# Norm factors of a two-layer diffusion block: from per-token columns to a product with ones on all partitions

## The chip, the cores and the metric

The kernel runs on one core of one Trainium2 chip. The metric is device time in microseconds (us), the median of several executions. A core has engines that run side by side: TensorE (PE, with PEld for its weight loads) multiplies matrices, VectorE (DVE) and ScalarE (ACT) work elementwise, GpSimd (POOL) does little here, and DMA queues move data between HBM and the on-chip SBUF. Matmul results land in PSUM. Each engine takes its own instructions strictly in the order of the program and waits on semaphores for the others.

## The reference

Two layers work on 256 tokens x and 256 context tokens ctx, 1024 features each. A layer is a half feed-forward, a block of four mixers, and a second half feed-forward; each starts with an RMS norm that is scaled and shifted by vectors from an adaLN product. In the second layer ctx ends after the mixers' states.

```python
def rms_norm(x, g):
    xf = x.astype(jnp.float32)
    y = xf * lax.rsqrt(jnp.mean(xf * xf, axis=-1, keepdims=True) + EPS)
    return (y * g.astype(jnp.float32)).astype(x.dtype)

def modulate(h, shift, scale):
    return h * (1 + scale) + shift

def half_ffn(h, shift, scale, gate, g, wi, wo):
    return h + 0.5 * gate * swiglu(modulate(rms_norm(h, g), shift, scale), wi, wo)

def hybrid_layer(x, ctx, c, c_ctx, p, last):
    ...
    x = half_ffn(x, sx[0], sx[1], sx[2], p['ffn1_norm'], p['ffn1_wi'], p['ffn1_wo'])
    ctx = half_ffn(ctx, sc[0], sc[1], sc[2], p['ffn1_norm'], p['ffn1_wi'], p['ffn1_wo'])
    u_x = modulate(rms_norm(x, p['mix_norm']), sx[3], sx[4]) @ p['w_in']
    ...
    x = x + sx[5] * mix_tokens(u_x, rows, dirs_x, states_x, p)
    x = half_ffn(x, sx[6], sx[7], sx[8], p['ffn2_norm'], p['ffn2_wi'], p['ffn2_wo'])
    if not last:
        ...
    return x, ctx
# after both layers: rms_norm(x, final_norm)
```

One of the four mixers, the convolution, ends in a layer norm over 256 channels, whose variance is computed in the same way as the RMS norms.

## The kernel before

Activations lie with features on the 128 partitions: `x` is 8 tiles `x[m]` of 128 features by 512 tokens, the first 256 (a half, S = 256) of x and the other 256 of ctx. Products need fp32 accuracy, so each operand is split into a high part in the format fp32r and a low part that holds the rest: weights `raw` into `whi` (a cast on ACT, L165) and `wlo` (a subtraction on DVE, L166), normed activations into `yh` and `yl`. A product is then three matmuls (`mm3`, L177 to L179): high by high, low by high, high by low. Weights stream through two buffers of 128 x 2048 for `whi` and two for `wlo`, so that a cast waits until the matmuls that read the buffer last are done.

A stage ends with projections that update `x`: `part` (L479) does one tile m for a range of tokens and adds it to `x[m]`. For 512 tokens `project` holds back the tile m = 6 (KT - 2) and then goes by halves: m = 6 and 7 for the first 256 tokens, then m = 6 and 7 for the second. Both tiles lie in one weight buffer.

After each update ACT squares `x[m]` (L374) and DVE adds it to the sum `ss` (L378). The next stage's norm needs the factor 1 / root(mean + EPS) per token on all partitions:

- `rstd` brings the sum over the partitions into columns, one token per partition, by small fp32 matmuls with a two-column operand `mean` (L391 for the tiles 0 to 6, L392 for the last square).
- `rsqrt_cols` (L204 to L215) does a root from an integer first guess and three Newton steps, on tiles of 128x1 and 128x2.
- `bcast` multiplies the identity by each column (`diag`, L225) and takes a product with ones (L227), which leaves the factor in PSUM on all partitions.
- `norm_scale` (L416) makes `ny` from `x`, the scale `gs` and the factor; `norm_shift` makes `yh` on ACT (L423) and `yl` on DVE (L424).

The first half's statistics are hooked into the second half's matmuls, after RA/8 of the tile m = 6 and, for the spread, after RB/8 of the tile m = 7; the second half's come behind. Where only 256 tokens are left (`early` in `ffn`, the last boundary), the first two up-projections use `z` = x times scale, and the factor comes in afterwards (`late_act`, `zg` and `zv`, L544 and L546).

Five such boundaries are spoken of below, by the time of the trace: I (first feed-forward to mixers, layer 0, 412 us), II (mixers to second feed-forward, 619), III (to layer 1, 987), IV (first feed-forward to mixers, layer 1, 1361) and V (the last one, 256 tokens, 1494).

In the mixers, the input weights come in groups of columns: `k` (keys, 8 x 128 columns, half a buffer), `vg` (values and gates, 8 x 288, of which seven fit a buffer and the last goes into tiles of its own, `rest`), `q` and more. `group` loads and splits them ahead of their turn (`prio`). Products with `fm` have features, those with `tm` tokens on the partitions. The order of the instructions on each engine is set when the program is built: a scheduler places them by priority and its own estimate of when they are ready, and it's fixed from then on. So code that changes in one place shifts what stands beside what in others.

## Time and profile before

| | us |
|---|---|
| median of 3 runs | 1705.04 (1703.88 to 1705.18) |
| profiled execution | 1703.85 |
| its span in the profile | 1702.1 |
| PE busy | 1678.8 |
| DVE busy | 1193.8 |
| ACT busy | 575.8 |

The span is what the profile covers; the execution's own time is 1.75 us longer. A row of a timeline gives start, duration, engine, line, operation, tiles and how many were merged, and in brackets how long the engine had been idle before it and what ended that. Matmuls are pipelined: a duration of 0.28 us includes the way through the array, while the next starts 0.12 us later. An fp32 matmul appears as two records. The granted clock is that of TensorE, 1.00 for its full level of 2.4 GHz and 0.50 for 1.2 GHz.

### The profile page before, as it was taken

The page shows a single profiled execution, that of the slowest core. Times are in us where ns is not written, and L with a number is a line of the kernel's source. Part 1 is how long each engine was busy: PE and PEld are TensorE (multiplying, and loading weights), DVE is VectorE, ACT ScalarE, POOL GpSimd, SP SyncE. Part 2 cuts the span into 40 slices and gives each one's busy share as a digit, 9 for nine tenths or more (in the row PEclk, how much of TensorE's full clock was granted, in tenths as well). Part 3 has the DMA queues.
Part 4 walks back from the last instruction along what each step waited for, and adds up shares of the span by engine and source line. Part 5 has one row for each costly group of instructions (what it writes and reads, how often), then busy time and mean ns, then how long its engine had stood idle before and what let it go on. Part 6 is the DMA issues. An engine that isn't in the chain of part 4 may idle for free.

```text
span 1702.1 us, 23539 instructions
## 1 busy us (share of the span) xinstructions
PE 1678.8 (99%) x9650; PEld 1440.4 (85%) x9650; DVE 1193.8 (70%) x2077; ACT 575.8 (34%) x737; POOL 33.6 (2%) x59
## 2 busy tenths in 40 slices
PE   8999999999999999999999999999999998999998
PEld 5888888878888898888888898888878897899998
DVE  5799866896675678888669776654464678775555
ACT  3322212333532443222122242221233254554343
POOL 0000000010000000000000000000000000000010
PEclk9999999999999999999999999999999999999999
DMA  9555644533232235545445425444433234344552
GB/s 370 185 188 182 211 157 153 180 121 104 102 105 85 95 129 180 183 163 183 166 148 193 165 104 194 166 155 149 151 124 106 86 130 162 110 157 177 179 195 79
DMA packets 51452, 262.55 MB, mean 154 GB/s; under 512 B 6010, under 2 KB 10944, under 8 KB 28816
## 3 DMA queue, kind: packets, MB, share of 16 engines
q1 hardware_dynamic: 49968, 257.05, 42.9%
q0 software_dynamic: 1376, 4.00, 0.6%
q8 instruction: 75, 1.23, 0.3%
q14 instruction: 33, 0.27, 0.0%
HBM read 257.88 MB, written 3.15 MB: 153 GB/s over the span
## 4 chain that ended last, share of the span: by engine, by line
PE 92%; DVE 3%; DMA 2%; ACT 1%; issue 1%; SPq 0%; POOL 0%; DVEq 0%; ACTq 0%; POOLq 0%
PE psm L177 29%; PE psm L178 28%; PE psm L179 28%; DVE acc L316 1%; ACT whi L165 1%; DVE wlo L166 1%; DMA adaw<-in_ada_w_dram 1%; DMA pm<-in_k_pool_dram 1%; PE psa L979 1%; DMA vec<-in_vecs_dram 1%; PE psa L1216 0%; PE psa L1038 0%; PE psa L1198 0%; PE psa L331 0%; PE psa L881 0%
## 5 line engine op out<-in xcount | busy, mean ns | idle before, releaser
L179 PE MATMUL psm<-yh,wlo 128*128 128x512 f32 (+1 forms) x1616 | 570.1, 354 | 2.5 <-DVE wlo L166 2.5
L177 PE MATMUL psm<-yh,whi 128*128 128x512 f32 (+1 forms) x1616 | 570.3, 355 | 1.4 <-DVE glu L776 0.9
L178 PE MATMUL psm<-yl,whi 128*128 128x512 f32 (+1 forms) x1616 | 571.1, 354 | 0.1
L165 ACT CAST whi<-raw 128x2048 fp32r<-128x2048 f32 (+3 forms) x172 | 304.1, 1770 | 599.8 <-PE psm L178 534.6
L166 DVE TENSOR_TENSOR wlo<-raw,whi 128x2048 fp32r<-128x2048 f32 (+3 forms) x172 | 363.7, 2116 | 133.6 <-ACT whi L165 133.3
L179 PEld LDWEIGHTS psm<-yh,wlo 128*128 128x128 f32 x1616 | 305.5, 189 | 46.5 <-DVE wlo L166 4.0
L177 PEld LDWEIGHTS psm<-yh,whi 128*128 128x128 f32 x1616 | 304.6, 189 | 46.3 <-issue 3.1
L178 PEld LDWEIGHTS psm<-yl,whi 128*128 128x128 f32 x1616 | 305.7, 189 | 42.5 <-DVE yl L424 0.9
L316 DVE SCALAR_TENSOR_TENSOR acc<-adaw,cvec,acc 128x512 f32<-128x512 f32 x392 | 274.5, 746 | 2.8
L177 PE MATMUL psm<-hh,whi 128*128 128x512 f32 (+1 forms) x752 | 265.1, 353 | 0.0
L179 PE MATMUL psm<-hh,wlo 128*128 128x512 f32 (+1 forms) x752 | 264.4, 352 | 0.0
L178 PE MATMUL psm<-hl,whi 128*128 128x512 f32 (+1 forms) x752 | 264.3, 351 | 0.0
L178 PEld LDWEIGHTS psm<-hl,whi 128*128 128x128 f32 x752 | 142.3, 189 | 19.4 <-DVE hl L166 0.4
L179 PEld LDWEIGHTS psm<-hh,wlo 128*128 128x128 f32 x752 | 142.3, 189 | 19.4 <-DVE acc L316 0.8
L177 PEld LDWEIGHTS psm<-hh,whi 128*128 128x128 f32 x752 | 142.2, 189 | 18.7 <-issue 0.2
L496 DVE TENSOR_TENSOR sg<-psm,sg 128x512 f32<-128x512 f32 (+1 forms) x90 | 54.3, 605 | 133.6 <-PE psm L179 119.6
L479 DVE SCALAR_TENSOR_TENSOR x<-psm,gt,x 128x256 f32<-128x256 f32 x112 | 50.4, 478 | 115.9 <-PE psm L179 115.8
L495 ACT ACTIVATE sg<-psm 128x512 f32<-128x512 f32 (+1 forms) x90 | 47.9, 532 | 215.7 <-PE psm L179 215.7
L374 ACT ACTIVATE sq<-x 128x512 f32<-128x512 f32 (+1 forms) x64 | 33.2, 523 | 90.9 <-DVE x L479 74.7
L177 PE MATMUL psm<-whi,yh 128*128 128x256 f32 (+1 forms) x200 | 58.1, 295 | 0.6 <-ACT whi L165 0.6
L178 PE MATMUL psm<-wlo,yh 128*128 128x256 f32 (+1 forms) x200 | 58.1, 294 | 0.0
L179 PE MATMUL psm<-whi,yl 128*128 128x256 f32 (+1 forms) x200 | 57.9, 293 | 0.0
(287 smaller groups left out, 1480.9 us busy)
## 6 DMA issues: line engine op xcount, KB each, us to landing
raw<-in_ffn_wi_dram SPq DMA_DIRECT2D x88, 1024.0 KB, 4.8
adaw<-in_ada_w_dram SPq DMA_DIRECT2D x66, 1024.0 KB, 5.1
raw<-in_ffn_wo_dram SPq DMA_DIRECT2D x32, 896.0 KB, 4.6
raw<-in_ffn_wo_dram SPq DMA_DIRECT2D x16, 1024.0 KB, 5.0
raw<-in_w_in_dram SPq DMA_DIRECT2D x14, 1024.0 KB, 4.8
raw<-in_w_out_dram SPq DMA_DIRECT2D x8, 1024.0 KB, 4.9
adaw<-in_ada_w_dram SPq DMA_DIRECT2D x24, 256.0 KB, 7.2
pm<-in_k_pool_dram SPq DMA_DIRECT2D x12, 256.0 KB, 3.1
```

Of the source, the lines that this page charges most:

```text
L165: self.nc.scalar.copy(hi[:, s], src[:, s])
L166: self.nc.vector.tensor_tensor(lo[:, s], src[:, s], hi[:, s].bitcast(F32), op=ALU.subtract)
L177: mm(ps, lhsT=ah, rhs=bh, start=first, stop=False)
L178: mm(ps, lhsT=ah, rhs=bl, start=False, stop=False)
L179: mm(ps, lhsT=al, rhs=bh, start=False, stop=last)
L316: nc.vector.scalar_tensor_tensor(acc, ws[half][:, k, :], sc, acc, op0=ALU.mult, op1=ALU.add)
L374: nc.scalar.activation(sq, self.x[m][:, lo:lo + n], AF.Square)
L479: nc.vector.scalar_tensor_tensor(self.x[m][:, s], ps[:, v * S - lo:v * S - lo + S], gate[v][:, m:m + 1], self.x[m][:, s], op0=ALU.mult, op ...
L495: nc.scalar.activation(sg, w[2][:, s], AF.Silu)
L496: nc.vector.tensor_tensor(sg, w[3][:, s], sg, op=ALU.mult)
L979: nc.tensor.matmul(ps[par], lhsT=fwd[:, 2 * i + par, :], rhs=cur[par], start=True, stop=True)
```

## The change

There are three parts.

1. The RMS factors. `sumsq` now adds the last square into `ss` too. `spread` takes the sum over the partitions by one fp32 product of ones (128x128) with `ss` (128x256), which leaves it on all partitions, and does the first guess and three Newton steps there on tiles of 128x256, eleven dependent DVE instructions (L402 to L407, the last into PSUM). The factor root(D) goes into the norms' vectors once (`self.norms`). `rstd` stays for the final norm. The first half is hooked in after RA/8 of the tile m = 6; the second hook is gone.
2. The convolution's variance: the two squares are added on DVE (`css`), and one matmul per 128 tokens is left of two.
3. The mixers' keys: `keys` loads the weights of `k` as before but splits them in two halves into four tiles `khi`, `klo` of 128x512 of the pool for activations. The value weights take the weight buffer in which the keys were.

```diff
@@ -35,7 +35,7 @@
 PRE = 400
 FSPLIT = 14
 F0 = (2.0, 0, 0.8, 16)
-RA, RB = 2, 4
+RA = 2
 PZ = 2
 F1 = (1.9, 0, 1)
 F2 = (0.8, 0, 1.0, 20)
@@ -240,6 +240,7 @@
                 v[name] = vt[:, l, at:at + c]
                 at += c
             self.vec.append(v)
+        self.norms = vt[:, :, 72:96]
 
 
     def ada_init(self, craw):
@@ -374,30 +375,37 @@
         nc.scalar.activation(sq, self.x[m][:, lo:lo + n], AF.Square)
         if m == 0:
             self.ss, self.rb = sq, {}
-        elif m < KT - 1:
+        else:
             nc.vector.scalar_tensor_tensor(self.ss[:, lo:lo + n], sq, EPS * D / P if m == 1 else 0.0, self.ss[:, lo:lo + n],
                                            op0=ALU.add, op1=ALU.add)
-        else:
-            self.last_sq = sq
 
     def rstd(self, lo, n):
 
         nc = self.nc
-        sq = self.last_sq
         nt = n // P
         ps = self.pa((P, nt, 2))
         for j in range(nt):
             a = lo + j * P
-            nc.tensor.matmul(ps[:, j, :], lhsT=self.ss[:, a:a + P], rhs=self.mean, start=True, stop=False)
-            nc.tensor.matmul(ps[:, j, :], lhsT=sq[:, j * P:j * P + P], rhs=self.mean, start=False, stop=True)
+            nc.tensor.matmul(ps[:, j, :], lhsT=self.ss[:, a:a + P], rhs=self.mean, start=True, stop=True)
         self.r = self.rsqrt_cols(ps, nt)
         return self.r
 
-    def spread(self, lo, r):
-
-        for i in range(r.shape[1] * P // S):
-            c = i * S // P
-            self.rb[lo // S + i] = self.bcast(r[:, c:c + S // P], S // P)
+    def spread(self, lo, n):
+
+
+        nc = self.nc
+        for v in range(lo // S, (lo + n) // S):
+            ps = self.pa((P, S))
+            nc.tensor.matmul(ps, lhsT=self.ones, rhs=self.ss[:, v * S:v * S + S], start=True, stop=True)
+            t = self.tmp((P, 2, S), name="root")
+            a, y = t[:, 0, :], t[:, 1, :]
+            nc.vector.tensor_single_scalar(a.bitcast(I32), ps.bitcast(I32), 1, op=ALU.logical_shift_right)
+            nc.vector.tensor_scalar(y.bitcast(I32), a.bitcast(I32), -1.0, float(0x5F3759DF), op0=ALU.mult, op1=ALU.add)
+            for i in range(3):
+                nc.vector.tensor_tensor(a, y, y, op=ALU.mult)
+                nc.vector.scalar_tensor_tensor(a, a, -0.5, ps, op0=ALU.mult, op1=ALU.mult)
+                nc.vector.scalar_tensor_tensor(ps if i == 2 else y, a, 1.5, y, op0=ALU.add, op1=ALU.mult)
+            self.rb[v] = ps
 
     def norm(self, l, name, T):
         yh = [self.yp.tile([P, T], F32R, tag="y", name=self.nm("yh")) for _ in range(KT)]
@@ -452,19 +460,11 @@
         elif m == KT - 2:
             self.held = (m, wh, wl, act, gate)
         else:
-            state = {}
-
-            def stats():
-                state["r"] = self.rstd(0, S)
-
-            def spread():
-                self.spread(0, state["r"])
-
             self.part(*self.held, 0, S, 3)
             self.part(m, wh, wl, act, gate, 0, S, 3)
-            self.part(*self.held, S, S, 3, {len(act) * RA // 8: stats})
-            self.part(m, wh, wl, act, gate, S, S, 3, {len(act) * RB // 8: spread})
-            self.spread(S, self.rstd(S, S))
+            self.part(*self.held, S, S, 3, {len(act) * RA // 8: lambda: self.spread(0, S)})
+            self.part(m, wh, wl, act, gate, S, S, 3)
+            self.spread(S, S)
 
     def part(self, m, wh, wl, act, gate, lo, w, last, hooks={}):
         nc = self.nc
@@ -480,10 +480,10 @@
                                            self.x[m][:, s], op0=ALU.mult, op1=ALU.add)
         if last:
             self.sumsq(m, lo, w)
-            if m == KT - 1 and last < 3:
-                r = self.rstd(lo, w)
-                if last == 1:
-                    self.spread(lo, r)
+            if m == KT - 1 and last == 1:
+                self.spread(lo, w)
+            elif m == KT - 1 and last == 2:
+                self.rstd(lo, w)
 
     def up_tiles(self, T):
         wh, wl = self.whl((P, 2 * KT, P))
@@ -697,10 +697,10 @@
 
         def fm(wg, c, n, TT, lo=0):
 
-            wh, wl = wg
+            wh, wl = (a if isinstance(a, list) else [a[:, k, :] for k in range(KT)] for a in wg)
             ps = self.ps((P, TT - lo))
             for k in range(KT):
-                self.mm3(ps[:n], wh[:, k, c:c + n], wl[:, k, c:c + n], yh[k][:, lo:TT], yl[k][:, lo:TT], k == 0, k == KT - 1)
+                self.mm3(ps[:n], wh[k][:, c:c + n], wl[k][:, c:c + n], yh[k][:, lo:TT], yl[k][:, lo:TT], k == 0, k == KT - 1)
             return ps
 
         sizes = {name: sum(n for _, n in segs) for name, segs in GROUPS.items()}
@@ -730,8 +730,20 @@
                 self.mm3(ps, yh[k][:, s], yl[k][:, s], wh[k], wl[k], k == 0, k == KT - 1)
             return ps
 
+        def keys():
+
+            with self.prio(-PRE):
+                raw = self.load(w[:, :KT * P].rearrange("p (k n) -> p k n", k=KT))
+                hi, lo = [], []
+                for i in range(0, KT, 4):
+                    hl = [self.h((P, 4, P), F32R, name) for name in ("khi", "klo")]
+                    self.split(*hl, raw[:, i:i + 4])
+                    for dst, a in zip((hi, lo), hl):
+                        dst += [a[:, k, :] for k in range(4)]
+            return hi, lo
+
         kk, gg, qq = self.h(name="k"), self.h((96, 512), F32R, name="g"), self.h((P, T), name="q")
-        wk, wv = group("k"), group("vg", PIECES)
+        wk, wv = keys(), group("vg", PIECES)
         vv = []
         for v in range(2):
             s = slice(v * S, v * S + S)
@@ -921,17 +933,16 @@
         for i in range(2):
             nc.tensor.matmul(mu, lhsT=self.ones, rhs=cacc[i], start=i == 0, stop=i == 1)
         yield
-        sqs = []
+        sqs = self.tmp((P, T), name="css")
         for i in range(2):
             nc.vector.scalar_tensor_tensor(cacc[i], mu, -1.0 / DG, cacc[i], op0=ALU.mult, op1=ALU.add)
-            sq = self.tmp((P, T), name="csq")
+            sq = sqs if i == 0 else self.tmp((P, T), name="csq")
             nc.scalar.activation(sq, cacc[i], AF.Square)
-            sqs.append(sq)
+        nc.vector.tensor_tensor(sqs, sqs, sq, op=ALU.add)
         n = T // P
         ps = self.pa((P, n))
         for j in range(n):
-            for i in range(2):
-                nc.tensor.matmul(ps[:, j:j + 1], lhsT=sqs[i][:, j * P:(j + 1) * P], rhs=self.ones[:, 0:1], start=i == 0, stop=i == 1)
+            nc.tensor.matmul(ps[:, j:j + 1], lhsT=sqs[:, j * P:(j + 1) * P], rhs=self.ones[:, 0:1], start=True, stop=True)
         yield
         rb = self.bcast(self.rsqrt(ps, n, 1.0 / DG), n)
         for i in range(2):
@@ -1271,7 +1282,7 @@
             self.warm_up()
             for m in range(KT):
                 self.sumsq(m, 0, 512)
-            r = self.rstd(0, 512)
+            self.spread(0, 512)
             yh = [self.yp.tile([P, 512], F32R, tag="y", name=self.nm("yh")) for _ in range(KT)]
             yl = [self.yp.tile([P, 512], F32R, tag="y", name=self.nm("yl")) for _ in range(KT)]
             up = [self.up_tiles(512) for _ in range(2)]
@@ -1300,8 +1311,8 @@
                 self.split(up[i][0][:, half[p]], up[i][1][:, half[p]], raws[i][:, half[p]])
 
             acc = [self.pa() for _ in range(2)]
+            nc.vector.tensor_scalar(self.norms, self.norms, D ** 0.5, None, op0=ALU.mult)
             self.gemv(ws[2], every, acc[0])
-            self.spread(0, r)
             self.ada_end(0, 2, self.ada_row(acc[0]))
             self.derive(0, [1], two, 0, 4)
             scale(first)
```

The change moves instructions. Three places, in the order that stands in the program:

DVE where the mixers of layer 0 end and the second feed-forward begins (619 us in the trace before), before the change; `x_120` is the tile m = 7, here its second half, whose update reads the last projection matmul; `psa_5218` holds the factor of the first half, `wlo_5365` are the weights of the second up-projection:

```order
L225 TENSOR_SCALAR diag_5219<-ident_99,sm_903_5178 128x128 x2
L378 SCALAR_TENSOR_TENSOR sq_4920<-sq_5202,sq_4920 128x256
L416 SCALAR_TENSOR_TENSOR ny_5290<-x_113,gs_2817,psa_5218 128x256
L416 SCALAR_TENSOR_TENSOR ny_5294<-x_114,gs_2817,psa_5218 128x256
L416 SCALAR_TENSOR_TENSOR ny_5298<-x_115,gs_2817,psa_5218 128x256
L424 SCALAR_TENSOR_TENSOR yl_5282<-ny_5290,mods_197,yh_5274 128x256
L479 SCALAR_TENSOR_TENSOR x_120<-psm_5205,mods_197,x_120 128x256
L416 SCALAR_TENSOR_TENSOR ny_5302<-x_116,gs_2817,psa_5218 128x256
L166 TENSOR_TENSOR wlo_5365<-raw_5370,whi_5364 128x1024
L204 TENSOR_SCALAR sm_910_5244<-psa_5239 128x2
L424 SCALAR_TENSOR_TENSOR yl_5283<-ny_5294,mods_197,yh_5275 128x256
```

The same place after it; `psa_5089` and `root_5091` belong to the first half, `psa_5154` and `root_5156` to the second:

```order
L407 SCALAR_TENSOR_TENSOR root_5091<-root_5091 128x256
L405 TENSOR_TENSOR root_5091<-root_5091 128x256
L479 SCALAR_TENSOR_TENSOR x_120<-psm_5125,mods_197,x_120 128x256
L406 SCALAR_TENSOR_TENSOR root_5091<-root_5091,psa_5089 128x256
L166 TENSOR_TENSOR wlo_5259<-raw_5264,whi_5258 128x1024
L407 SCALAR_TENSOR_TENSOR psa_5089<-root_5091 128x256
L379 SCALAR_TENSOR_TENSOR sq_4854<-sq_5151,sq_4854 128x256
L424 SCALAR_TENSOR_TENSOR ny_5184<-x_113,gs_2790,psa_5089 128x256
L424 SCALAR_TENSOR_TENSOR ny_5188<-x_114,gs_2790,psa_5089 128x256
L402 TENSOR_SCALAR root_5156<-psa_5154 128x256
L432 SCALAR_TENSOR_TENSOR yl_5176<-ny_5184,mods_197,yh_5168 128x256
L403 TENSOR_SCALAR root_5156<-root_5156 128x256
```

Before, three `ny` and a `yl` of the first half stood ahead of the last update of `x_120` and the weight split behind them; now that update stands ahead of the root's last two steps, the weight split ahead of the last one, and the first `ny` comes three rows behind the split. The second half's root then stands in turns with `ny` and `yl` of the first.

PE at the same place, first before (`psm_5205` is the last projection, `psm_5356` and `psm_5357` the first up-projection), then after (`psm_5125`, and `psm_5250` on):

```order
L179 MATMUL psm_5205<-mh_4883,wlo_5085 128x256
L391 MATMUL psa_5239<-mean_102,sq_4920 128x2
L177 MATMUL psm_5356<-yh_5274,whi_5354 128x256
L177 MATMUL psm_5357<-yh_5274,whi_5354 128x256
L178 MATMUL psm_5356<-yl_5282,whi_5354 128x256
L179 MATMUL psm_5356<-yh_5274,wlo_5355 128x256
```

```order
L179 MATMUL psm_5125<-mh_4817,wlo_5019 128x256
L399 MATMUL psa_5154<-sq_4854,ones_100 128x256
L177 MATMUL psm_5250<-yh_5168,whi_5248 128x256
L177 MATMUL psm_5251<-yh_5168,whi_5248 128x256
L177 MATMUL psm_5260<-yh_5168,whi_5258 128x256
L177 MATMUL psm_5261<-yh_5168,whi_5258 128x256
L178 MATMUL psm_5250<-yl_5176,whi_5248 128x256
```

One small matmul stood between the stages, and the others of the second half (L392, L391, L392) some way behind it; now the product with ones for the second half's `ss` stands there whole.

DVE at the last boundary (1511 us in the trace before), where the up-projections `zg`, `zv` of `z` get their factor and `wlo_12744` or `wlo_12541` is a later weight tile, before and after:

```order
L416 SCALAR_TENSOR_TENSOR ny_12487<-x_120,gs_10042,psa_12413 128x256
L424 SCALAR_TENSOR_TENSOR yl_12457<-ny_12483,mods_198,yh_12449 128x256
L424 SCALAR_TENSOR_TENSOR yl_12458<-ny_12487,mods_198,yh_12450 128x256
L544 TENSOR_TENSOR zg_12592<-psm_12493,rb_12518 128x256
L546 TENSOR_TENSOR zv_12593<-psm_12494,rb_12518 128x256
L166 TENSOR_TENSOR wlo_12744<-raw_12749,whi_12743 128x2048
L547 SCALAR_TENSOR_TENSOR zv_12593<-zv_12593,sh_12541,zg_12592 128x256
```

```order
L424 SCALAR_TENSOR_TENSOR ny_12284<-x_120,gs_9896,psa_12202 128x256
L166 TENSOR_TENSOR wlo_12541<-raw_12546,whi_12540 128x2048
L432 SCALAR_TENSOR_TENSOR yl_12253<-ny_12276,mods_198,yh_12245 128x256
L544 TENSOR_TENSOR zg_12389<-psm_12290,rb_12315 128x256
L432 SCALAR_TENSOR_TENSOR yl_12254<-ny_12280,mods_198,yh_12246 128x256
L546 TENSOR_TENSOR zv_12390<-psm_12291,rb_12315 128x256
L432 SCALAR_TENSOR_TENSOR yl_12255<-ny_12284,mods_198,yh_12247 128x256
```

The split of 128x2048 stood behind `zg` and `zv`, and now it stands ahead of both, with three `yl` still to come.

## Rows read from the trace of the kernel before

**Rows 1.** The page: span, engines, chain by engine

```profile
span 1702.1 us, 23539 instructions
...
PE 1678.8 (99%) x9650; PEld 1440.4 (85%) x9650; DVE 1193.8 (70%) x2077; ACT 575.8 (34%) x737; POOL 33.6 (2%) x59
...
PE 92%; DVE 3%; DMA 2%; ACT 1%; issue 1%; SPq 0%; POOL 0%; DVEq 0%; ACTq 0%; POOLq 0%
```

**Rows 2.** Groups of PE by shape: xcount | busy us, mean ns | idle before

```profile
L392 PE MATMUL psa<-mean,sq 128*128 128x2 f32 x48 | 8.7, 250 | 1.2 <-ACT sq L374 1.2
...
L391 PE MATMUL psa<-mean,sq 128*128 128x2 f32 x48 | 7.8, 232 | 0.0
...
L934 PE MATMUL psa<-ones,csq 128*128 128x1 f32 x24 | 2.9, 240 | 0.0
```

**Rows 3.** Timeline of PE at the first half's statistics, boundary I

```profile
405.26 0.28 PE L391 MATMUL psa<-mean,sq 128*128 128x2 f32 x2
...
405.61 0.28 PE L178 MATMUL psm<-hl,whi 128*128 128x256 f32 x1
405.73 0.28 PE L179 MATMUL psm<-hh,wlo 128*128 128x256 f32 x1
```

**Rows 4.** Timeline of PE, an fp32 product of 256 columns

```profile
332.80 1.89 PE L671 MATMUL psa<-eo,dft 128*128 128x256 f32 x8
```

**Rows 5.** Groups of DVE by shape

```profile
L416 DVE SCALAR_TENSOR_TENSOR ny<-x,gs,psa 128x256 f32<-128x256 f32 x88 | 38.1, 474 | 5.8 <-PE psa L227 5.6
...
L166 DVE TENSOR_TENSOR wlo<-raw,whi 128x1024 fp32r<-128x1024 f32 x16 | 19.5, 1222 | 3.8 <-ACT whi L165 3.7
...
L652 DVE TENSOR_SCALAR rinv<-psa 128x256 f32<-128x256 f32 x4 | 1.7, 424 | 2.3 <-PE psa L650 2.3
```

**Rows 6.** Timeline of DVE at boundary II

```profile
618.22 1.26 DVE L416 SCALAR_TENSOR_TENSOR ny<-x,gs,psa 128x256 f32<-128x256 f32 x3 [0.26 <-PE psa L227]
...
619.79 0.48 DVE L479 SCALAR_TENSOR_TENSOR x<-psm,mods,x 128x256 f32<-128x256 f32 x1
```

**Rows 7.** Timeline of ACT at boundary II

```profile
618.73 0.51 ACT L423 ACTIVATE yh<-ny,mods 128x256 fp32r<-128x256 f32 x1 [1.24 <-DVE ny L416]
619.53 1.05 ACT L165 CAST whi<-raw 128x1024 fp32r<-128x1024 f32 x1 [0.29 <-PE psm L178]
```

**Rows 8.** Timeline of PE at boundary II

```profile
619.33 0.28 PE L179 MATMUL psm<-mh,wlo 128*128 128x256 f32 x1
...
619.60 0.48 PE L177 MATMUL psm<-yh,whi 128*128 128x256 f32 x2
```

**Rows 9.** Timeline of PE at boundary I and behind it

```profile
411.51 0.28 PE L179 MATMUL psm<-hh,wlo 128*128 128x256 f32 x1
...
412.91 0.53 PE L177 MATMUL psm<-whi,yh 128*128 128x288 f32 x2 [0.29 <-ACT whi L165]
414.04 0.38 PE L392 MATMUL psa<-mean,sq 128*128 128x2 f32 x2 [0.61 <-ACT sq L374]
...
435.39 0.39 PE L177 MATMUL psm<-yh,whi 128*128 128x512 f32 x1
```

**Rows 10.** Stretches: us, busy us of each engine, granted clock, DMA

```profile
414.00:416.00 2.00, 1.96 (x11) 1.96 (x12) 2.00 (x7) 1.19 (x3) 0.00 (x0) 0.64 0.00 0
416.00:418.00 2.00, 2.00 (x10) 2.00 (x10) 2.00 (x11) 0.51 (x1) 0.00 (x0) 0.51 0.91 266
1388.00:1470.00 82.00, 74.11 (x677) 65.00 (x677) 66.75 (x154) 40.44 (x68) 1.05 (x2) 1.00 0.47 163
```

**Rows 11.** Timeline of PE at boundary V

```profile
1494.33 0.28 PE L391 MATMUL psa<-mean,sq 128*128 128x2 f32 x2
...
1511.89 0.39 PE L177 MATMUL psm<-yh,whi 128*128 128x256 f32 x1 [0.25 <-DVE zg L544]
```

**Rows 12.** Timeline of DVE at the start and at boundary V

```profile
34.51 0.23 DVE L293 TENSOR_TENSOR mods<-psa,vec 128x4 f32<-128x4 f32 x2 [5.72 <-PE psa L291]
...
1501.62 1.27 DVE L416 SCALAR_TENSOR_TENSOR ny<-x,gs,psa 128x256 f32<-128x256 f32 x3 [1.02 <-PE psa L227]
```

## The prediction

> **What bounds the kernel now.** I read the page first: PE is busy 99% of the span, and 92% of the chain that ended last is PE [rows 1]. So work taken from PE comes off the end, and a stretch in which PE waits is added to it. DVE is busy 70%; its time counts only where PE waits for it. Then I read groups of instructions, for the price of what goes [rows 2 to 4] and of what comes [rows 5], and last the places where a new norm starts, in order of time [rows 6 to 12].
>
> There are five such places besides the start. Four have 512 tokens in two halves: boundary I (first feed-forward of layer 0 to its mixers, 411.6 us), II (mixers to second feed-forward, 619.5), III (layer 0 to layer 1, built like II) and IV (like I, in layer 1). V is the last, with 256 tokens (1494 us).
>
> Call Z the moment at which PE has issued the last projection matmul of the old stage. At II that matmul starts at 619.33 and the first of the new stage at 619.60 [rows 8]: no wait. DVE began the first ny at 618.22, ahead of the last x update at 619.79 [rows 6], so the first half's factor was ready before Z. At I PE lost more: 0.29 us for a cast, 0.61 for a square, and then the granted clock was 0.64 and 0.51 for two stretches of 2 us [rows 9, 10].
>
> **The change on PE.** Of the 48 small matmuls of the norms 46 go. Each is two records; such a pair moves the next matmul from 405.26 to 405.61, less the 0.12 us that one matmul of 256 columns takes (405.61 to 405.73): 0.23 us [rows 3]. The convolution mixer saves half of its 24 records [rows 2], 6 matmuls at about 0.22: 1.3 us. Of 28 bcast matmuls of 128 columns 22 go, and 11 products with ones of 256 columns come: 1.89 us for four of that kind, 0.47 each at most [rows 4]. By equal columns the 11 cost what the 22 did, so I cost them at nothing; at most it is 11 x 0.47 = 5.2 against nothing. So PE does four times 0.23 = 0.9 us less per 256 tokens: 1.8 at each of I to IV, 0.9 at V, 1.8 at the start (where PE is idle anyway), and with the convolution and two of the final norm 9.9 us outside the start.
>
> **The change on DVE.** Per 256 tokens about 17 short instructions go and eleven of 128x256 come, each waiting for the one before. No row shows this chain. The nearest are one source out of PSUM at 0.42 us (L652) and two sources at 0.47 (L416) [rows 5]: alone, eleven are 4.6 to 5.2 us, and I take 4.9. Laid between independent instructions a step costs only the distance of starts, (1.26 - 0.47) / 2 = 0.39 for the dearer kind [rows 6]; I take 0.36, 4.0 for eleven.
>
> **What becomes late.** The first half's product with ones is issued after 13 matmuls of the second half, some 4.6 us before Z. Its root would need 4.9 alone, and DVE has an x update and a sum between its steps. So at Z two steps are left, and DVE's program puts the last x update (which waits for Z) ahead of one and a split of weights ahead of the other, as the rows under the change show. That split waits for a cast on ACT, and the cast for the weight buffer that the old stage's last matmul frees. By the rows of II, from Z = 619.45: x update at 0.34 [rows 6]; cast 0.1 to 1.15 [rows 7]; split 1.2 to 2.4 [rows 5]; last step of the root to 2.85; first ny at 3.1, with a sum between. From ny to PE is 1.0 us, ny 0.47 and yh 0.51 [rows 5, 7]. PE starts the new stage at Z + 4.1. Meanwhile it does one product with ones (0.43), so it waits 3.7 us where it waited for nothing at II and III.
>
> Then DVE must give y at PE's pace. From 2.4 on it has the step and the sum (0.7), sixteen ny and yl (6.3), the eleven steps of the second half's root (4.0) that the program lays between them, and one ny more and a second split (1.5): the eighth yl comes at 14.9 and the matmuls behind it end at 16. PE's own work is 96 x 0.12 = 11.5, so 15.6 at the earliest. I take 16.2, for small waits; before, it was 13.1 (11.5, 1.3 of the second half's statistics and bcast, 0.3 of waits).
>
> After a wait of 3.7 us PE's clock should fall, as it did at I behind waits of 0.9 us in all: (0.36 + 0.49) x 2.0 = 1.7 us of work lost in 414:418 [rows 10]. Some of that falls on time in which PE is short of y anyway, so I take 1.2 at II and III. Against it stands the mixers' stretch 1388:1470, where PE lay idle 7.9 of 82 us in small pieces and the granted clock stayed 1.00 [rows 10]; if no clock falls, the sum below is 5 instead of 9.
>
> The Trainium skill (TensorE: Matmul & The Clock Gate, "Part 1: The HAM clock gate") says that the array's clock follows how busy it has been lately and that half rate is where it goes when it was idle. The trace agrees at I, at 0.51 of full clock. By that rule alone all five waits are followed by half clock at full price, and the sum would be 10.
>
> **The sum**, against the profiled execution:
> - II, III: 16.2 + 1.2 - 13.1, less 0.9 saved ahead of Z: +3.4 each, +6.8. Bounds +1.6 and +4.0 each.
> - I, IV: these have waits and a half clock already; the value part ends 23.8 us after Z (411.63 to 435.39 [rows 9]). After: DVE's last yl starts at 2.4 + 0.7 + 12.1 + 4.0 + 0.5 = 19.7, ends at 20.1, and 33 matmuls of 0.12 to 0.135 (288 columns) stand behind it: 24.3. PE's own way is 4.1, its 144 matmuls of 19.2 and 1.7 of clock: 25.0. Less 0.9: +0.3 each, +0.6. The keys' earlier split and the value split ahead of Z are in this, since they leave no other wait at Z; alone they would save the wait of 0.29 and part of the 0.61. Bounds -1.4 and +1.0 each.
> - V: the root starts when DVE has done both splits (cast 1.15, split 2.4, sum and z 3.1, split 4.3 after Z), takes 4.9 alone and waits 0.2 for a copy in it: ny at 9.4, before 7.3 (1494.33 to 1501.62 [rows 11, 12]). A weight split of 2.2, ten ny and yl and the next weight split, which now stands ahead of zg, put zg at 19.3. PE's next matmul needs the PSUM buffer that zg reads, as at 1511.89 [rows 11]: 19.8 against 17.6, +2.2, and 0.8 for a clock that may fall: +3.0. Bounds +1 and +4.
> - Convolution -1.3; its added sum on DVE (0.4 to 0.7 us, twice) lies under PE's other matmuls, and without that cover costs 1.1.
> - End: one more sum on DVE (0.4), two small matmuls fewer: +0.2.
> - Start: the root on 512 tokens takes DVE some 5 us more, but DVE lies idle 5.7 us ahead of 34.51, until PE's adaLN products come [rows 12]: 0, without that cover +5. Bounds -0.5 and +1.
>
> Sum +9.3. The profiled execution took 1703.85 us (span 1702.1 and 1.75 around it); the median of the runs is 1705.04, 1.19 more. So 1713.2 by the profiled one and 1714 as a median.
>
> **Rivals.**
> A. The removed PE work comes off and the waits don't grow: faster. For it: PE bounds 99%, and I and IV have waits of their own to lose. Against it: x update, cast and split stand ahead of the root's last step in the program, 3 us whatever else. If the cast found its buffer free before Z, PE would wait 1.4 instead of 3.7 at four places and no clock would fall: 9.3 - 9.2 - 3.2 = -3.1, 1702. If V's wait went too (-2.2): 1700; with PE waiting 1 us a place, 1698. The kernel gets faster from a wait of about 2.2 us per boundary downwards.
> B. The waits are there, but no clock falls and DVE keeps pace: II and III 15.6 - 13.1 - 0.9 = +1.6 each, I and IV 4.1 + 19.2 - 23.8 - 0.9 = -1.4 each, V +1.5, the rest -1.1: +0.8, 1706, no change.
> C. More than forecast: steps cost 0.48 even where laid between others (eleven times 0.12, 1.3 at four places), and every wait brings twice the loss of clock (0.8 more at five): 9.3 + 5.2 + 4.0, 1723.
>
> **Chances.** The forecast 0.62 (its own range 1708 to 1718), A 0.13, B 0.17, C 0.08. About 0.2% (3.4 us) is what a measurement of this kernel can tell from no change. Slower by more: forecast and C, 0.70; within it: B and a little of A, 0.18; faster: the rest of A, 0.12. For 80% the range goes from 1700 to 1720.
>
> **What would show it.** Around 619 and 987 PE waits some 3.7 us, ended by the first yh, with a weight split and the root's last step (line 407) just ahead on DVE, and the granted clock is half in the 4 us behind; at 1511 PE waits some 3.5 us for zg; at 412 one wait of 3.7 stands in place of two short ones. The 1388 to 1470 stretch is as it was. If the first ny at II starts less than 1 us after Z, or PE's idle time in all stays near the 23.3 us of now (1702.1 - 1678.8), the forecast is wrong and A holds; if PE waits as said and the clock stays at 1.00, it is B.

## The result

The changed kernel takes 1720.86 us (median), the kernel before 1704.59 beside it: 1.0091 times, with a 95% interval of 1.0077 to 1.0104. It is slower, as forecast, by 16 us where 9 were forecast, and its median lies 0.86 us above the forecast's range of 1700 to 1720. One of its four executions took 5295.21 us, which no trace explains; the ratio leaves it out, and the other three took 1719.91 to 1721.81 with a median of 1719.91, at the upper end of that range but above the forecast's own 1708 to 1718. The profiled execution took 1719.91 us, its span 1718.1.

The page of the changed kernel (span; busy time by engine; the chain that ended last, by engine), against [rows 1]:

```profile
span 1718.1 us, 23244 instructions
...
PE 1677.1 (98%) x9524; PEld 1433.8 (83%) x9524; DVE 1219.8 (71%) x2030; ACT 577.2 (34%) x739; POOL 33.6 (2%) x59
...
PE 89%; DVE 7%; DMA 2%; ACT 1%; issue 1%; SPq 0%; DVEq 0%; ACTq 0%
```

PE is busy 1.7 us less and the span is 16.0 longer, so PE stands idle for 41.0 us where it was 23.3; in the chain DVE has 4 points more. (The forecast took 9.9 us of work off PE outside the start. Busy time also holds what half clock adds: behind II matmuls of 256 columns start 0.21 us apart at half clock, from 624.39 to 624.60, and 0.12 apart at full.)

Where the time went shows best stage by stage. An update of x on DVE (line 479) waits for PE's projection, so its start is a landmark that both traces have (the last one of a stage, some 0.2 to 0.4 us behind Z, stands for Z here):

| stretch between x updates | before | after | difference | forecast |
|---|---|---|---|---|
| start, to the first update | 202.38 | 202.73 | +0.35 | 0 |
| to Z of I | 209.59 | 208.66 | -0.93 | -0.9 |
| I: Z to Z of II | 207.82 | 208.14 | +0.32 | -0.35 |
| II: Z to the first update behind it | 166.86 | 170.48 | +3.62 | +4.3 |
| to Z of III | 200.39 | 199.85 | -0.54 | -0.9 |
| III | 165.01 | 169.60 | +4.59 | +4.3 |
| to Z of IV | 208.79 | 208.40 | -0.39 | -0.9 |
| IV and layer 1's mixers | 117.69 | 119.31 | +1.62 | +0.55 |
| V, to the last stage's first update | 108.75 | 115.61 | +6.86 | +3.0 |
| the end (rest of the span) | 114.79 | 115.36 | +0.57 | +0.2 |

(The forecast is the prediction's sum, shared out by stretch: 0.9 ahead of each Z, half of the convolution's 1.3 to each layer.) II and III together came near their terms. V costs 3.9 us more than its term; that is more than half of the 6.7 us that are missing.

Boundary II of the changed kernel, DVE by time of start (start, us, then the instruction; in brackets the idle time ahead and what ended it), where [rows 6] have the first ny ahead of the x update:

```profile
619.53 0.48 DVE L479 SCALAR_TENSOR_TENSOR x<-psm,mods,x 128x256 f32<-128x256 f32 x1
619.93 0.41 DVE L406 SCALAR_TENSOR_TENSOR root<-root,psa 128x256 f32<-128x256 f32 x1
620.32 1.22 DVE L166 TENSOR_TENSOR wlo<-raw,whi 128x1024 fp32r<-128x1024 f32 x1
621.46 0.43 DVE L407 SCALAR_TENSOR_TENSOR psa<-root 128x256 f32<-128x256 f32 x1
621.80 0.42 DVE L379 SCALAR_TENSOR_TENSOR sq<-sq,sq 128x256 f32<-128x256 f32 x1
622.13 0.86 DVE L424 SCALAR_TENSOR_TENSOR ny<-x,gs,psa 128x256 f32<-128x256 f32 x2
```

PE there, against [rows 8]:

```profile
619.04 0.28 PE L179 MATMUL psm<-mh,wlo 128*128 128x256 f32 x1
622.27 0.70 PE L399 MATMUL psa<-sq,ones 128*128 128x256 f32 x2 [2.95 <-DVE sq L379]
623.20 1.17 PE L177 MATMUL psm<-yh,whi 128*128 128x256 f32 x4 [0.23 <-ACT yh L431]
```

Z is 619.16. The first ny starts at Z + 2.97 (forecast 3.1), PE's new stage at Z + 4.04 (forecast 4.1). The same wait of 2.95 stands at 414.13 (I), 992.60 (III) and 1370.60 (IV). Behind it the clock falls. Stretches of II, III and V (us, busy time of PE, PEld, DVE, ACT, POOL, then granted clock, DMA share, GB/s):

```profile
619.00:623.00 4.00, 1.02 (x5) 0.41 (x3) 3.96 (x9) 2.66 (x4) 0.00 (x0) 1.00 0.01 2
623.00:627.00 4.00, 3.80 (x19) 3.80 (x20) 3.99 (x12) 1.57 (x4) 0.00 (x0) 0.57 0.00 0
991.00:995.00 4.00, 2.40 (x7) 1.70 (x8) 3.47 (x9) 1.77 (x3) 0.00 (x0) 0.62 0.00 0
995.00:999.00 4.00, 4.00 (x21) 4.00 (x22) 4.00 (x12) 1.08 (x3) 0.00 (x0) 0.53 0.01 4
1521.00:1525.00 4.00, 0.20 (x1) 0.20 (x2) 3.30 (x5) 2.38 (x6) 0.00 (x0) 0.93 0.03 6
1525.00:1529.00 4.00, 4.00 (x18) 3.76 (x19) 2.90 (x9) 1.67 (x5) 0.00 (x0) 0.50 0.72 260
1529.00:1533.00 4.00, 4.00 (x27) 4.00 (x27) 0.43 (x1) 0.57 (x2) 0.00 (x0) 0.72 0.00 0
```

At III half clock lasts through two stretches, at II through one, and III costs 1 us more, 4.59 against 3.62. That is this execution's, not the place's: e3 and e7 below have the same order of instructions at II and III, and there they cost 3.8 and 4.1 us (e3) and 4.0 and 3.7 (e7). DVE is full (3.96 to 4.00 of 4) at II: it has no slack to give PE y sooner.

Boundary V, all engines by time of start, against [rows 11, 12]:

```profile
1512.75 1.26 DVE L424 SCALAR_TENSOR_TENSOR ny<-x,gs,psa 128x256 f32<-128x256 f32 x3
...
1519.55 0.28 PE L179 MATMUL psm<-z,wlo 128*128 128x256 f32 x1
1519.79 1.90 ACT L165 CAST whi<-raw 128x2048 fp32r<-128x2048 f32 x1 [0.97 <-PE psm L178]
1521.72 2.29 DVE L166 TENSOR_TENSOR wlo<-raw,whi 128x2048 fp32r<-128x2048 f32 x1 [0.70 <-ACT whi L165]
1523.93 0.48 DVE L432 SCALAR_TENSOR_TENSOR yl<-ny,mods,yh 128x256 fp32r<-128x256 f32 x1
1524.33 0.42 DVE L544 TENSOR_TENSOR zg<-psm,rb 128x256 f32<-128x256 f32 x1
1524.80 0.58 PE L177 MATMUL psm<-yh,whi 128*128 128x256 f32 x1 [4.97 <-DVE zg L544]
```

This is a ring. PE waits for zg, zg stands behind a split on DVE, the split waits for a cast on ACT, and the cast waits for the weight buffer that PE's own last z matmul (1519.55) frees. From that matmul to the next PE does nothing for 4.97 us: cast 1.9, split 2.2, a yl 0.4, zg to PE 0.5. DVE stood idle for only 0.70 of them, since its own ny and yl had just been done. It starts whenever PE has finished, however early the factor is: e8 and e9 below show that.

### The profile page after: what moved, and what is told of

The parts are those of the page before. It is cut to its first block, busy times and chain, and to the rows that moved or that the text cites. A ratio compares the mean times of both kernels' runs of the same rounds, so it can differ in the third digit from the quotient of the medians.

```text
span 1718.1 us, 23244 instructions
## 1 busy us (share of the span) xinstructions
PE 1677.1 (98%) x9524; PEld 1433.8 (83%) x9524; DVE 1219.8 (71%) x2030; ACT 577.2 (34%) x739; POOL 33.6 (2%) x59
## 4 chain that ended last, share of the span: by engine, by line
PE 89%; DVE 7%; DMA 2%; ACT 1%; issue 1%; SPq 0%; DVEq 0%; ACTq 0%
PE psm L177 28%; PE psm L178 27%; PE psm L179 27%; DVE wlo L166 1%; DVE acc L317 1%; ACT whi L165 1%; DMA adaw<-in_ada_w_dram 1%; DMA vec<-in_vecs_dram 1%; PE psa L990 1%; PE psa L1049 0%; DVE root L405 0%; PE psa L1227 0%; DMA pm<-in_k_pool_dram 0%; DVE root L406 0%; DVE sq L379 0%
## 5 line engine op out<-in xcount | busy, mean ns | idle before, releaser
L177 PE MATMUL psm<-yh,whi 128*128 128x512 f32 (+1 forms) x1584 | 562.2, 358 | 5.4 <-DVE zg L544 5.0
L179 PE MATMUL psm<-yh,wlo 128*128 128x512 f32 (+1 forms) x1584 | 562.7, 357 | 2.5 <-DVE wlo L166 2.5
L178 PE MATMUL psm<-yl,whi 128*128 128x512 f32 (+1 forms) x1584 | 563.4, 357 | 0.0
L177 PEld LDWEIGHTS psm<-yh,whi 128*128 128x128 f32 x1584 | 300.5, 191 | 50.9 <-DVE zg L544 5.2
L179 PEld LDWEIGHTS psm<-yh,wlo 128*128 128x128 f32 x1584 | 301.6, 191 | 46.6 <-DVE wlo L166 4.0
L178 PEld LDWEIGHTS psm<-yl,whi 128*128 128x128 f32 x1584 | 301.9, 191 | 41.6 <-DVE yl L432 0.3
```

The lines of the kernel that those rows point to most:

```text
L177: mm(ps, lhsT=ah, rhs=bh, start=first, stop=False)
L178: mm(ps, lhsT=ah, rhs=bl, start=False, stop=False)
L179: mm(ps, lhsT=al, rhs=bh, start=False, stop=last)
```

## The experiments

Ratios are against runs of the kernel before on the same chip (its medians 1704.3 to 1705.4). First the three parts, each put alone into the kernel before.

**e1, the key tiles alone.**

```diff
...
-        wk, wv = group("k"), group("vg", PIECES)
+        wk, wv = keys(), group("vg", PIECES)
```

> The kernel before with the third part alone (keys' weights in four tiles of the activations' pool, split ahead of the boundary; the value weights in the freed buffer). Theory: it removes the wait of 0.29 us for a cast at boundaries I and IV and part of the 0.61 behind it, and with them perhaps the half clock there: -1 to -4 us against before. Rival: the waits at I and IV move to the query weights, which now stand in the last buffer: within 1 us of before.

1701.85 us, 0.9983 [0.9974, 0.9992]. The two waits of [rows 9] and the low clock behind them are gone; PE's only wait at I, and the stretch:

```profile
417.66 0.39 PE L178 MATMUL psm<-yl,khi 128*128 128x256 f32 x1 [0.28 <-DVE yl L424]
```

```profile
412.00:416.00 4.00, 3.94 (x33) 3.71 (x32) 3.54 (x9) 2.37 (x6) 1.19 (x3) 1.00 0.08 16
```

The stretches of I and IV are 2.4 and 2.5 us shorter than before (the start is 2.4 longer in that execution; it lay between 202.3 and 206.6 us over the study's profiles, without a pattern by kernel). So this part is a gain by itself, which the norm factors take back; its size is the median's 2.4 us, since single executions differ by as much. How much of it is the waits and how much the clock was not taken apart: in e9, whose order at I is that of the kernel before, the clock stayed whole behind the same two waits (0.30 and 0.60 us), and the stretch I was 1.6 us shorter.

**e2, the convolution's one column alone.**

```diff
...
-            sqs.append(sq)
+        nc.vector.tensor_tensor(sqs, sqs, sq, op=ALU.add)
...
```

> The kernel before with the second part alone (the convolution's two squares added on DVE, 6 small matmuls fewer). Theory: the six matmuls come off the end, -1.3 us. Rival: the sum on DVE and ACT's squares in a row delay PE at the mixers' end by as much: 0 or slower by up to 1 us.

1703.13 us, 0.9992 [0.9983, 1.0001]: about 1.1 us less, by its interval not told from nothing. The two mixer stretches are 0.85 and 0.56 shorter in its profile, which fits the forecast's 1.3 but does not show it.

**e3, the norm factors alone** (spread and sumsq as in the diff above, keys and convolution as before).

> The kernel before with the first part alone (factors by the product with ones and the root on all partitions). Theory: the whole loss is in this part: 1721 to 1723, all five boundary waits as after the whole change. Rival: a part of the loss comes from the keys' and value weights being split ahead of boundaries I and IV, so that this one is 2 us or more faster than the whole change.

1723.44 us, 1.0107 [1.0091, 1.0122]: this part costs 19 us, more than the whole change.

**e4, one small matmul per 128 tokens, factors still by columns** (in the kernel before, with e2's edit).

```diff
-        elif m < KT - 1:
+        else:
...
-            nc.tensor.matmul(ps[:, j, :], lhsT=self.ss[:, a:a + P], rhs=self.mean, start=True, stop=False)
-            nc.tensor.matmul(ps[:, j, :], lhsT=sq[:, j * P:j * P + P], rhs=self.mean, start=False, stop=True)
+            nc.tensor.matmul(ps[:, j, :], lhsT=self.ss[:, a:a + P], rhs=self.mean, start=True, stop=True)
```

> The kernel before with the convolution's part and, of the norms' part, only the sum: the last square is added into the sum on DVE, so that one small matmul per 128 tokens is left of two; columns, the root on 128x1 tiles and bcast stay. Theory: what hurts is the length of the root on 128x256 behind the last sum, not the added sum (0.42 us): faster than before by the 12 + 6 matmuls of about 0.22 us outside the start, less some waiting at the boundaries: -2 to -4 us. Rival: any lengthening of the chain behind the last square, 0.4 us, is paid by PE at four or five boundaries: 0 to +2 us.

1718.19 us, 1.0076 [1.0062, 1.0090]: a gain was expected, and it lost 14 us, without the root on 128x256: 3.8 at II, 3.8 at III and 6.5 at V. At V there is the same wait, to the digit:

```profile
1522.20 0.58 PE L177 MATMUL psm<-yh,whi 128*128 128x256 f32 x1 [4.97 <-DVE zg L540]
```

At II the split of the second up-projection's second half stands at 634.14, behind all but one of the second half's ny and yl (in the kernel before it starts at 628.44, among them), and PE runs dry, in waits of 0.17 us for each yl and at last 0.52 for the split; DVE and PE there:

```profile
633.74 0.48 DVE L420 SCALAR_TENSOR_TENSOR yl<-ny,mods,yh 128x256 fp32r<-128x256 f32 x1
634.14 1.22 DVE L166 TENSOR_TENSOR wlo<-raw,whi 128x1024 fp32r<-128x1024 f32 x1
...
635.41 0.50 PE L179 MATMUL psm<-yh,wlo 128*128 128x256 f32 x2 [0.52 <-DVE wlo L166]
```

So a small edit moves the program's order elsewhere, and it looks as if the order alone could cost more than what was edited. e7, e9 and e11 test that.

**e5, the x update of tile 7 behind the root's last step** (changed kernel, I to IV).

```diff
...
+            with self.after(self.first) if last == 3 and m == KT - 1 and lo else nullcontext():
...
```

> The changed kernel with one order set on DVE: at boundaries I to IV the last x update is put behind the last step of the first half's root (the weight split then falls behind it too). The work is the same. Theory: PE's wait of about 3 us at each is the root's last step standing behind x update, cast and split; now the root ends some 0.9 us earlier and the first ny with it, so PE starts the new stage 1.1 to 1.3 us earlier at four places: -4 to -6 us, more where the clock then falls less. Rival: DVE's whole load in the 15 us behind the boundary sets the pace (32 ny and yl, 11 steps), then an earlier start is given back within the stage: within 2 us of the changed kernel.

1732.16 us, 1.0161 [1.0145, 1.0176]: some 12 us worse than the change, where 4 to 6 better were expected. PE starts the new stage at Z + 2.84 instead of 4.04, but the order moved too, as in e4: both halves of the second up-projection's split now stand behind all of the norm, PE does the product with ones behind its first three matmuls, where DVE waits 1.05 us for it, and II loses 8.6 us. PE and DVE at II:

```profile
624.18 1.01 PE L177 MATMUL psm<-yh,whi 128*128 128x256 f32 x3 [2.68 <-ACT yh L431]
...
640.66 2.35 DVE L166 TENSOR_TENSOR wlo<-raw,whi 128x1024 fp32r<-128x1024 f32 x2
...
641.94 0.51 PE L179 MATMUL psm<-yh,wlo 128*128 128x256 f32 x2 [0.63 <-DVE wlo L166]
```

What the update's place is worth by itself is not shown by this run.

**e6, PE kept at work in the wait** (changed kernel; six fp32 products of 256 columns at I to IV).

```diff
...
+            for _ in range(FILL):
+                self.nc.tensor.matmul(fill, lhsT=self.ones, rhs=self.x[KT - 2][:, S:], start=True, stop=True)
```

> The changed kernel with six more fp32 products of 128x256 on PE at each of boundaries I to IV, put between the last projection and the product with ones (their result is not used): about 2.6 us of work in a wait of 2.95. The waits for DVE stay. Theory: the half clock behind the waits costs time of its own, 1 to 3 us at II and III; with PE busy in the wait the granted clock stays at 1.00 and the kernel gets 3 to 6 us faster although it does 10 us more work on PE. Rival: the half clock falls on time in which PE is short of y anyway and costs nothing: the same within 1 us, or slower.

1720.25 us, 1.0091 [1.0076, 1.0106]: as the change. The clock is whole at II, and nothing is won; PE, then stretches:

```profile
620.55 2.75 PE L470 MATMUL psa<-x,ones 128*128 128x256 f32 x12
623.67 0.70 PE L400 MATMUL psa<-sq,ones 128*128 128x256 f32 x2 [0.36 <-DVE sq L380]
```

```profile
623.00:627.00 4.00, 3.41 (x22) 2.56 (x21) 3.99 (x12) 1.33 (x3) 0.00 (x0) 1.00 0.00 0
...
631.00:635.00 4.00, 3.46 (x25) 2.85 (x24) 4.00 (x10) 1.31 (x3) 0.00 (x0) 1.00 0.00 0
```

II costs 3.62 us with the filler and 3.62 without. At full clock PE catches up with DVE, which is full, and waits for y again (631 to 635). At III it costs 3.61, 1.0 less than in the changed kernel's profile; but e7 has 3.74 there without a filler, so this is no more than what executions of one order differ by. So the clock's term at II was covered by DVE's pace, as the prediction half allowed.

**e7, the fourth cast and split behind zg and zv** (changed kernel, V alone).

```diff
...
+                    with self.after(self.late):
+                        nc.scalar.copy(w[0], raw)
+                        nc.vector.tensor_tensor(w[1], raw, w[0].bitcast(F32), op=ALU.subtract)
...
```

> The changed kernel with one order set at boundary V: the cast and split of the fourth up-projection's weights are put behind zg and zv of the first. Theory: PE's wait of 4.97 us for zg is a ring: zg stands behind that split on DVE, the split waits for the cast, the cast for the buffer that PE's last z matmul frees, and PE waits for zg. Without it zg comes 2.6 us earlier: -2.5 us, and up to -6 if the 6.8 us of half clock behind it go. Rival: V is bound by the root's length and the eight ny and yl behind it, and the split only fills DVE's idle time: within 1 us of the changed kernel.

1716.62 us, 1.0071 [1.0056, 1.0086]: by the ratios 3.4 us won, and V's stretch is 4.0 shorter. V now costs 2.89 us. That this is the forecast's 3.0 is chance, since the forecast had the split ahead of zg. PE there:

```profile
1523.45 0.39 PE L177 MATMUL psm<-yh,whi 128*128 128x256 f32 x1 [2.37 <-DVE zg L544]
```

**e8, two Newton steps** (changed kernel; a less exact factor).

```diff
-            for i in range(3):
+            for i in range(2):
...
```

> The changed kernel with two Newton steps in place of three in the root on 128x256 (left out: the third, so the factors are less exact): eight dependent instructions in place of eleven. Theory: the chain's length decides, since with eight the first half's factor is ready about at the end of the last projection and the scheduler puts ny ahead of the last x update: PE's waits at I to IV shrink from 3 us to 1 or less and the half clocks with them; at V everything is 1.4 us earlier. -9 to -14 us. Rival: each root costs DVE time that PE pays for in proportion, three eighths of a part: -1.4 us at five places, about -6.

1719.47 us, 1.0085 [1.0068, 1.0102]: about 1 us won of 9 to 14, less than the intervals can tell. PE's wait at II halves, but the split slides back as in e4, and II and III cost 4.8 us each. At V PE's wait of 4.97 stays, and it goes on at Z + 21.8 as in the changed kernel: the root is shorter, but the ring is not. PE and DVE at II:

```profile
622.21 0.74 PE L177 MATMUL psm<-yh,whi 128*128 128x256 f32 x4 [1.43 <-ACT yh L431]
...
637.92 1.22 DVE L166 TENSOR_TENSOR wlo<-raw,whi 128x1024 fp32r<-128x1024 f32 x1
```

**e9, V's order of the change put into the kernel before**, which keeps its own factors.

```diff
...
+                    for f in (2, 3):
+                        soon[f] = self.whl((P, 2 * KT, P))
+                        self.split(*soon[f], self.load(wi[f]))
+                    late = self.mark(mybir.EngineType.DVE)
...
+                    with self.after(late):
+                        late_act(ws[0], cs[0], rb)
```

> The kernel before, with its own norm factors, and one thing of the changed kernel at boundary V: cast and split of the fourth up-projection's weights stand ahead of the first zg on ACT and DVE. Theory: V's price is the ring (zg behind a split, the split behind a cast, the cast behind PE's last z matmul), not the late factor. By the rows of the kernel before, the cast runs from 1511.6 to 1513.5, the split to 1515.7, zg to 1516.2, so PE waits 4.3 to 4.7 us where it waits 0.25 now, and then loses 1.7 to 2.6 us to half clock: +6 to +7, 1710 to 1711.5. Rival: the root's late end makes the wait and the order alone is cheap: at most +1.5, 1704 to 1706.

1710.12 us, 1.0037 [1.0022, 1.0051]: 5.4 us lost by this order alone, V's stretch 6.1 longer. All engines:

```profile
1512.48 0.28 PE L179 MATMUL psm<-z,wlo 128*128 128x256 f32 x1
1512.72 1.90 ACT L165 CAST whi<-raw 128x2048 fp32r<-128x2048 f32 x1 [1.06 <-issue]
1514.65 2.29 DVE L166 TENSOR_TENSOR wlo<-raw,whi 128x2048 fp32r<-128x2048 f32 x1 [2.74 <-ACT whi L165]
1516.86 0.42 DVE L548 TENSOR_TENSOR zg<-psm,rb 128x256 f32<-128x256 f32 x1
1517.33 0.58 PE L177 MATMUL psm<-yh,whi 128*128 128x256 f32 x1 [4.58 <-DVE zg L548]
```

DVE stood idle 2.74 us ahead of the split: it was not late, the cast was, and that by PE. The ring is V's price; the late factor is not needed for it.

**e10, the kernel before with the key tiles and the convolution's column** (the edits of e1 and e2).

> The kernel before with the key tiles and the one column of the convolution mixer, norm factors as before. If the two gains add (2.4 and 1.1 us): 1700.9. If the second is hidden by waits in the mixers: 1701.9, as the key tiles alone.

1699.68 us, 0.9971 [0.9960, 0.9982]: 5.1 us below before, where e1 and e2 alone gave 2.4 and 1.1: within their intervals the gains add, and this is faster than the kernel before and the changed one.

**e11, e4 with both orders put right.**

```diff
...
-        yh, yl = ys or self.norm(l, name, T)
+        yh, yl = ys or self.norm(l, name, T, 1)
...
                 ws = done or [up(0, PZ if early else 1), up(1, PZ if early else PIECES)]
+                for k in range(KT) if T > S and not ys else []:
+                    self.norm_part(l, name, k, 1, yh, yl)
...
```

(The last argument of norm is the number of halves that it writes, so the up-projections' splits now come ahead of the second half's norm; V's edit is that of e7.)

> The kernel of e4 (sums closed on DVE, one small matmul per 128 tokens, factors by columns) with two places of DVE's order put back to what the kernel before has: at II and III the second half of the second up-projection's split ahead of the second half's ny and yl, at V the fourth split behind zg and zv. Theory: e4's loss (3.8 us at II, 3.8 at III, 6.6 at V) is PE running out of split weights, by order alone: II and III fall to 1 us or less each, V to 3 or less, 1705 to 1709. Rival: one more sum on DVE at every boundary makes the statistics late, whatever the order: 1714 or more.

1704.70 us, 1.0000 [0.9991, 1.0009]: 13.5 us back, a little more than expected. II and III cost 0.3 us each, V 0.2. DVE at II and PE at V:

```profile
631.04 1.21 DVE L166 TENSOR_TENSOR wlo<-raw,whi 128x1024 fp32r<-128x1024 f32 x1
632.17 0.47 DVE L420 SCALAR_TENSOR_TENSOR yl<-ny,mods,yh 128x256 fp32r<-128x256 f32 x1
```

```profile
1514.73 0.39 PE L177 MATMUL psm<-yh,whi 128*128 128x256 f32 x1 [0.75 <-DVE zg L540]
```

So e4's loss was order, but for some 0.8 us at these three places.

**e12, e11 with the key tiles** (the edit of e1).

> The kernel of e11 with the key tiles besides. If the parts add, 2.4 us below e11: 1703 to 1706. If the order at II, III and V comes out wholly as before, the small matmuls saved on PE (half of them, about 1 us per boundary) show too and it goes below the key tiles alone: under 1701. Rival: as e4, 1714 or more.

1701.71 us, 0.9980 [0.9971, 0.9989]: between the two ranges. The keys' 2.4 us add (3.0 below e11), but the small matmuls saved do not show beyond that. It is no better than e1, and e10 stays the fastest.

**e13, the changed kernel with both orders put right** (the edits of e7 and e11).

> The changed kernel with both orders that e11 put right: at II and III the second half of the second up-projection's split ahead of the second half's ny and yl, at V the fourth cast and split behind zg and zv (as in e7, 1716.6). If the wait of 2.95 us for the root at II and III and what follows it is the loss there: 1715.5 to 1717.5, as e7. If the order of the split is most of it, as in e4 against e11 (3.5 us at each of II and III): 1709 to 1711.

1718.60 us, 1.0081 [1.0065, 1.0096]: above both ranges and no better than e7. II and III cost 4.6 and 4.9 us (half clock lasted longer than in e7's profile, with 4.0 and 3.7), where both orders cost 0.3 each without the root on 128x256 (e11). At II the wait is what it was:

```profile
622.99 1.22 PE L399 MATMUL psa<-sq,ones 128*128 128x256 f32 x2 [2.95 <-DVE sq L379]
```

With three steps II and III are the root's, not the order's. That wait is for the sum, which stands behind the root's last step.

**e14, e13 with two Newton steps** (the edit of e8).

> As e13, with two Newton steps instead of three (a less exact factor). In e8 this made PE's wait at II and III 1.43 us instead of 2.95 and left the clock whole, and yet lost 4.8 us at each. If that loss was the split's order, II and III fall to some 2 us each and V to 3 or less: 1709 to 1712. If it was DVE's own work in the stretch: 1714 to 1716.

1707.01 us, 1.0009 [1.0000, 1.0019]: below the range of either theory. II, III and V cost 1.5, 1.5 and 0.6 us. PE at II:

```profile
618.29 0.74 PE L177 MATMUL psm<-yh,whi 128*128 128x256 f32 x4 [1.43 <-ACT yh L431]
```

The shorter root pays only where the order lets it: about 1 us without (e8), 11.6 with (from e13).

## Why the prediction was right in its sign and short in its size

- **The root's lateness at I to IV: right.** The wait's length, its place, what stands ahead of the root's last step, and that the clock falls behind it came as worked out, to 0.1 us in the starts. (What ended the 2.95 was the last sum, for the product with ones, and yh only the 0.23 behind it.) At V a step of the root starts 0.46 us behind the one that it waits for, and at II 0.33 behind an independent one (forecast 0.45 and 0.36):

```profile
1510.00 0.42 DVE L405 TENSOR_TENSOR root<-root 128x256 f32<-128x256 f32 x1
1510.46 0.42 DVE L406 SCALAR_TENSOR_TENSOR root<-root,psa 128x256 f32<-128x256 f32 x1
```

```profile
624.34 0.42 DVE L405 TENSOR_TENSOR root<-root 128x256 f32<-128x256 f32 x1
624.67 0.47 DVE L424 SCALAR_TENSOR_TENSOR ny<-x,gs,psa 128x256 f32<-128x256 f32 x1
```

- **II and III: the sum is near, two of its terms are not.** They cost 8.2 us together from Z against 8.6, and e13 beside e11 shows that the root is their cause. But the 8.6 hold 1.2 for the clock at each, and at II the clock cost nothing (e6): there the stage itself took 3.62 us more where 16.2 - 13.1 = 3.1 were worked out. That the errors cancel is luck.
- **The step that failed is V's term,** "A weight split of 2.2, ten ny and yl and the next weight split, which now stands ahead of zg, put zg at 19.3". It saw the split in the program's order, but laid it on DVE as 2.2 us of work following on. The split can't start before a cast that waits for PE's own last z matmul (Z + 16.6 by the trace, with Z = 1502.97), and with a cast of 1.9, the split and a yl that alone puts zg at Z + 21.4, where it came. DVE's own way was mis-sized too, though not what decided: the first ny came at Z + 9.8 (forecast 9.4), and fourteen ny and yl, not ten, stand ahead of zg and took 6.5 us where the sum leaves 5.5, so that DVE waited only 0.70 for the cast. PE was held 4.3 us longer than before instead of 2.2. The clock then cost 2.6 instead of 0.8: by then most of y was ready, and PE was the limit (the rows of 1525 to 1533 lose (0.50 + 0.28) x 4.0 = 3.1 us of work). Together +6.9 for +3.0. e9 has the ring without the root (+6.1), e7 the root without the ring (+2.9).
- **Saved ahead of Z: too much at two places.** 0.9 was forecast per boundary; the stretch to I gave 0.93, those to III and IV 0.54 and 0.39. Two times 0.4 us.
- **The clock.** It fell at all five boundaries of the changed kernel, to 0.57 at II and 0.50 at V. The Trainium skill (TensorE: Matmul & The Clock Gate, "Part 1: The HAM clock gate") says that half rate is the state of an array that was idle. The trace agrees in so far as PE had stood idle for 2.95 to 4.97 us ahead of each fall; that a like wait need not be followed by one is shown below (e9, e14). The fall cost nothing at II (e6), up to 1.0 us at III in the one profile where it lasted longer, and 2.6 at V.
- **The rivals.** B, that no clock falls, is out; so is A, since none of the forecast waits went. C's time is near, but not its mechanism: a step laid between others costs 0.33, not 0.48, and a dearer clock was met at V alone. Two sums are loose: B has V at +1.5, where its term without the clock is 2.2, and half clock at full price at all five (1.7 each) would make 11, not 10.
- **Still open:** 0.7 us at I and 1.1 at IV with layer 1's mixers over their terms. No run took them apart.

## What to carry to other kernels

Where an engine waits for a result that is queued behind another job, follow that job's own inputs back: if one of them is a buffer that the waiting engine frees, the wait is the whole ring (here 1.9 + 2.2 + 0.9 us), whatever the late result costs. When a scheduler or priorities set the order, compare the order at every boundary after an edit, not only where the edit is: e4 lost 14 us and e11 got 13.5 back with the same arithmetic. And test the parts of a change one by one: two of these three parts made the kernel with the lowest median of this study (e10, 5 us below before), and the third hid it.

## What the runs showed of the hardware

- Half clock can cost nothing: at II the granted clock was 0.57 for 4 us, and with the clock held at 1.00 the stage took as long (e6), since DVE set the pace.
- The length of a wait did not decide whether the clock fell. In e14 PE waited 1.43 us at II and at I; at II the clock stayed at 1.00, at I it was 0.57 in the 4 us behind. In the kernel before it was 0.64 and 0.51 [rows 10] behind the waits of [rows 9]; in e9, with the same order and the same waits, it stayed at 1.00. Behind waits of 2.95 us it fell at II in the change (0.57), e7 (0.60) and e13 (0.50). PE at I in e14 and the stretch behind, then the stretch behind the waits at I in e9:

```profile
412.22 0.39 PE L177 MATMUL psm<-yh,khi 128*128 128x256 f32 x1 [1.43 <-ACT yh L431]
```

```profile
414.00:418.00 4.00, 4.00 (x21) 4.00 (x21) 4.00 (x13) 1.02 (x2) 0.00 (x0) 0.57 0.87 299
```

```profile
416.00:420.00 4.00, 4.00 (x33) 4.00 (x34) 4.00 (x19) 1.55 (x5) 0.00 (x0) 1.00 0.47 143
```

- On DVE an operation of 128x256 that waits for the one before starts 0.46 us after it; with an independent one between them each takes 0.33 to 0.40.
